# One of the last stores of a rotary-score kernel moved to a GpSimd transfer on fifteen DMA engines

## The chip, the cores and the metric

The kernel runs on one core of a Trainium2 chip. The metric is the device time of one execution in microseconds, as the median of several runs. A profile's span is about 2 us shorter than the time of the same run (797.1 against 798.9 for the kernel before).

## The reference

```python
# q, k: [16, 512, 16, 64] float32; cos, sin: [512, 32] float32
q_rot = concat([q1*cos - q2*sin, q1*sin + q2*cos])      # k_rot likewise
scores = np.einsum('bshd,bthd->bsht', q_rot, k_rot)     # [16, 512, 16, 512] float32
```

The output is 268 MB, the inputs 67 MB. The kernel has 64 steps, and each step makes 4 MB of the output: 128 rows of 32 KB from step 4 on, and the first four steps in quarters.

## The kernel before

The kernel plans all its instructions itself, with the waits worked out from keys that each instruction reads and writes. Three stage tiles of 4 MB take the scores. They lie in SBUF, on the chip, each over 128 partitions. ScalarE copies eight pieces per step into one, then SyncE stores it in one DMA transfer of 128 partitions (the code here and below is cut, with # ... where lines are left out):

```python
    NST_BUFS = 3
    stage = [pool.tile([P, H, S], fp32, name=f"st{n}") for n in range(NST_BUFS)]
    o_v = out.rearrange("b (p c) h t -> b c p h t", c=C)
    # ... in scores(i, p):
        plan.add(ACT, one(lambda: nc.scalar.copy(out=so, in_=si)), [("ps", y)], [("st", s, p)])
        # ...
        elif b > 0 and p == HP - 1:
            dma(SP, nc.sync, o_v[b, i % C], st, f"out{s}", reads=[("st", s, x) for x in range(HP)])
```

Four of the loads of q are already "relieved": 120 of their rows go through GpSimd on the fifteen DMA engines other than number 4, which is slower than the rest (1,246 ns for a row of 32 KB against 1,213 while compute runs; the prediction shows how it was found). A tiny transfer of five rows goes ahead of them, meant to move GpSimd's cursor past engine 4. In the trace, from 480 to 504 us, fifteen chains of packets then carry the 8 KB pieces, sixteen each, and the slow engine's chain carries none. Each row is named as two halves in reversed order. The last eight rows go on other transfers.

```python
    RELIEVED = {("q", 5): 0, ("q", 8): 1, ("q", 11): 2, ("q", 14): 3}
    SLOW = 4
    # ... in load(which, b):
        def halves(lo, hi, keys, sem):
            src = bass.AP(d.tensor, d.offset + lo * E + F, [(E, hi - lo), (-F, 2), (1, F)])
            # ... dst in the same form
            dma(POOL, nc.gpsimd, dst, src, sem, writes=keys)

        plan.add(POOL, None, (), rows)           # waits, then resets GpSimd's cursor
        if x % 2:
            move_cursor(8)
            halves(n, P, rest, f"rest{x}")       # eight odd rows, meant for engines 8 to 15
        move_cursor(SLOW + 1)
        halves(0, n, rows, f"part{x}")           # 120 rows on the engines other than 4
        if not x % 2:
            dma(SP, nc.sync, t[n:]..., d[n:], sem, writes=rest)   # or by SyncE, meant for engines 0 to 7
```

The trace names no engine, so the numbers are my count: 4 is the slow one, 0 to 7 are the eight that an 8-row transfer of SyncE uses, 8 to 15 the other eight. What the trace shows is that the 8-row load issued at 482.17 ended in eight increments, from 504.22 to 508.93 us, the last of them 0.6 us after the slow engine's for the store ahead (508.33), so I take the slow engine to be one of the eight. Which the others are was not shown.

## Time and profile before

| what | value |
|---|---|
| time, median of 3 runs | 798.52 us (797.91 to 799.9) |
| span of the profile | 797.1 us |
| busy: PE, ScalarE, VectorE, GpSimd | 86%, 71%, 68%, 1% |
| DMA queues of SyncE and of GpSimd, share of 16 engines' span | 96.5% and 2.4% |
| last four stores issued at | 745.83, 754.27, 763.51, 773.23 us |
| last increment of the last store | 794.86 us |

The prediction below shows the lines. A "last increment" is the last of the increments that a transfer makes on its semaphore (the last store made sixteen, from 786.93 to 794.86 us; I take each to be one engine's). The trace keeps every one of them, and every DMA packet with its queue, size and duration. It does not keep the engine's number.

### The profile page before, as it was taken

The numbers are of one execution on the slowest core, as the hardware profiler recorded it, in microseconds if no ns is written. First come the engines' busy times: TensorE is split into PE (matmuls) and PEld (weight loads), VectorE is DVE, ScalarE is ACT, GpSimd is POOL, SyncE is SP. The second block draws the span as 40 slices with busy tenths as digits, with TensorE's granted clock in tenths as the row PEclk, the third lists the DMA queues.
The fourth block names the chain that finished last, engine by engine and source line by source line (L and its number), as shares of the span: only waits on it lengthen the run. The fifth ranks groups of instructions, "written<-read, shape, count | busy, mean of one in ns | idle before, by whom it ended". The sixth has DMA issues, their size and how long they took to land.

```text
span 797.1 us, 8197 instructions
## 1 busy us (share of the span) xinstructions
PE 684.3 (86%) x3072; PEld 295.4 (37%) x3072; DVE 545.2 (68%) x516; ACT 562.4 (71%) x647; POOL 8.4 (1%) x18
## 2 busy tenths in 40 slices
PE   3989999897989979799797988979989699789960
PEld 2444443343333434344342433334334244334420
DVE  6999988575775868568585767757758488575400
ACT  3978886785767858578585866768667677678860
POOL 0000000000000000100000000000000100000000
PEclk9999999898998989989898999989989899899995
DMA  8999999999999999999999999999999999999995
GB/s 346 420 424 433 429 418 434 426 434 423 430 413 427 435 434 428 439 421 414 426 427 437 432 435 426 419 428 432 428 431 433 432 429 411 428 432 437 430 433 238
DMA packets 18513, 335.87 MB, mean 421 GB/s; under 512 B 2128, under 2 KB 3408, under 8 KB 4432
## 3 DMA queue, kind: packets, MB, share of 16 engines
q1 hardware_dynamic: 16832, 327.42, 96.5%
q0 software_dynamic: 1376, 8.13, 2.4%
q10 hardware_dynamic: 288, 0.13, 0.1%
q8 instruction: 6, 0.10, 0.0%
q14 instruction: 11, 0.09, 0.0%
HBM read 67.24 MB, written 268.44 MB: 421 GB/s over the span
## 4 chain that ended last, share of the span: by engine, by line
DMA 47%; PE 35%; DVE 8%; ACT 6%; issue 1%; ACTq 0%; DVEq 0%; SPq 0%
DMA out_dram<-st 47%; PE ps L409 27%; PE bank L360 9%; ACT st L418 6%; DVE st L335 3%; DVE part L335 2%; DVE k_sb L335 2%; DVE q_sb L335 1%; DMA st<-in_k_dram 1%; DVE kT L378 0%; DVE qT L378 0%; ACTq L110 0%; DVEq L110 0%; SPq L542 0%; SPq L513 0%
## 5 line engine op out<-in xcount | busy, mean ns | idle before, releaser
L418 ACT COPY st<-ps 128x1024 f32<-128x1024 f32 x512 | 495.5, 1018 | 196.7 <-DMA out_dram<-st 103.3
L409 PE MATMUL ps<-kT,qT 64*128 64x512 f32 x2048 | 542.9, 646 | 71.6 <-ACT st L418 71.6
L409 PEld LDWEIGHTS ps<-kT,qT 64*128 64x128 f32 x2048 | 182.0, 195 | 261.0 <-issue 134.2
L378 DVE COPY qT<-bank 128x512 f32<-128x512 f32 x118 | 81.6, 691 | 197.3 <-PE bank L360 197.3
L360 PEld LDWEIGHTS bank<-ident,q_sb 128*128 128x128 f32 x480 | 54.7, 150 | 101.5 <-issue 99.5
L360 PE MATMUL bank<-ident,q_sb 128*128 128x128 f32 x480 | 85.5, 305 | 1.0 <-DVE q_sb L335 1.0
L360 PEld LDWEIGHTS bank<-ident,k_sb 128*128 128x128 f32 x480 | 50.4, 141 | 94.5 <-DVE k_sb L335 43.1
L360 PE MATMUL bank<-ident,k_sb 128*128 128x128 f32 x480 | 78.6, 287 | 1.6 <-DVE k_sb L335 0.8
L378 ACT COPY kT<-bank 128x512 f32<-128x512 f32 x122 | 72.5, 597 | 6.7 <-PE bank L360 6.7
L335 DVE TENSOR_TENSOR part<-q_sb,ss_t 128x1024 f32<-128x1024 f32 x60 | 73.5, 1225 | 3.2
L335 DVE TENSOR_TENSOR k_sb<-k_sb,part 128x1024 f32<-128x1024 f32 x60 | 73.5, 1225 | 2.1
L335 DVE TENSOR_TENSOR k_sb<-k_sb,cos_t 128x1024 f32<-128x1024 f32 x60 | 73.5, 1225 | 2.0
L335 DVE TENSOR_TENSOR q_sb<-q_sb,cos_t 128x1024 f32<-128x1024 f32 x60 | 73.5, 1225 | 2.1
L335 DVE TENSOR_TENSOR part<-k_sb,ss_t 128x1024 f32<-128x1024 f32 x60 | 73.0, 1216 | 0.3
L335 DVE TENSOR_TENSOR q_sb<-q_sb,part 128x1024 f32<-128x1024 f32 x60 | 72.9, 1216 | 0.0
L360 PE MATMUL bank<-ident,st 128*128 128x128 f32 x64 | 10.8, 319 | 13.2 <-DVE st L335 13.2
L360 PEld LDWEIGHTS bank<-ident,st 128*128 128x128 f32 x64 | 8.2, 161 | 18.5 <-DVE st L335 16.7
L335 DVE TENSOR_TENSOR part<-st,ss_t 128x1024 f32<-128x1024 f32 x8 | 9.8, 1222 | 6.4 <-DMA st<-in_k_dram 6.0
L335 DVE TENSOR_TENSOR st<-st,part 128x512 f32<-128x512 f32 x16 | 11.1, 691 | 0.5
L237 POOL DMA_DIRECT2D scratch<-in_q_dram x6 | 3.6, 600 | 615.4 <-PE bank L360 615.4
L335 DVE TENSOR_TENSOR st<-st,cos_t 128x1024 f32<-128x1024 f32 x8 | 9.8, 1225 | 0.3
L378 ACT COPY qT<-bank 128x512 f32<-128x512 f32 x10 | 5.7, 615 | 3.5 <-PE bank L360 3.5
(11 smaller groups left out, 11.0 us busy)
## 6 DMA issues: line engine op xcount, KB each, us to landing
out_dram<-st SPq DMA_DIRECT2D x60, 4096.0 KB, 25.5
k_sb<-in_k_dram SPq DMA_DIRECT2D x15, 2048.0 KB, 27.1
q_sb<-in_q_dram SPq DMA_DIRECT2D x11, 2048.0 KB, 29.2
out_dram<-st SPq DMA_DIRECT2D x16, 1024.0 KB, 13.3
q_sb<-in_q_dram POOLq DMA_DIRECT2D x4, 1920.0 KB, 32.6
st<-in_k_dram SPq DMA_DIRECT2D x1, 1536.0 KB, 9.0
st<-in_q_dram SPq DMA_DIRECT2D x1, 1536.0 KB, 12.2
st<-in_k_dram SPq DMA_DIRECT2D x1, 512.0 KB, 5.0
```

The source lines that it names most:

```text
L237: plan.add(engine, one(lambda: e.dma_start(dst, src)), reads, writes, sem=sem, also=also)
L335: plan.add(DVE, one(lambda: nc.vector.tensor_tensor(o, a, b, op=op)), reads, writes, also=more)
L360: done = [nc.tensor.transpose(bank[:, x, :], srcs[x], ident) for x in range(4)]
L378: plan.add(engine, one(lambda: copy(out=dst, in_=src)), [("bank", m)], keys)
L409: nc.tensor.matmul(out=ps[:, r, :], lhsT=lhs[lo:hi, :], rhs=rhs[lo:hi, :], start=True, stop=True)
L418: plan.add(ACT, one(lambda: nc.scalar.copy(out=so, in_=si)), [("ps", y)], [("st", s, p)])
```

## The change

The intent is to spare engine 4 its share of one late store, since one engine, taken to be number 4, finishes the last store 3.59 us after all the others (794.86 against 791.27). The store of step 62, the last but one, takes the form of the relieved loads.

```diff
+        elif p == HP - 1 and i == NST - 2:
+            n, F, o = 120, H * S // 2, o_v[b, i % C]
+            keys = [("st", s, x) for x in range(HP)]
+            plan.add(POOL, None, keys[:2], ())
+            move_cursor(SLOW + 1)
+            v = st[:n].rearrange("p h t -> p (h t)")
+            src = bass.AP(v.tensor, v.offset + F, [(v.ap[0][0], n), (-F, 2), (1, F)])
+            dst = bass.AP(o.tensor, o.offset + F, [(o.ap[0][0], n), (-F, 2), (1, F)])
+            dma(POOL, nc.gpsimd, dst, src, "out_part", reads=keys)
+            dma(SP, nc.sync, o[n:], st[n:], f"out{s}", reads=keys)
         elif b > 0 and p == HP - 1:
```

(`move_cursor` also moves out of `load`, unchanged.)

More of the change, by code (lines that the diff above doesn't have):

```diff
@@ L262, with move_cursor @@
     SLOW = 4
+    def move_cursor(k):
+        y = tiny[0]
+        tiny[0] += 1
+        src = bass.AP(q.tensor, 512 * y, [(512, k), (64, 2), (1, 2)])
+        dst = scratch[:k, 4 * y : 4 * y + 4].rearrange("p (a b) -> p a b", a=2)
+        dma(POOL, nc.gpsimd, dst, src, "cursor", writes=[("scratch", y)])
     def load(which, b):
@@ L280, in load @@
         d = dram[which][b]
-        def move_cursor(k):
-            y = tiny[0]
-            tiny[0] += 1
-            src = bass.AP(q.tensor, 512 * y, [(512, k), (64, 2), (1, 2)])
-            dst = scratch[:k, 4 * y : 4 * y + 4].rearrange("p (a b) -> p a b", a=2)
-            dma(POOL, nc.gpsimd, dst, src, "cursor", writes=[("scratch", y)])
         def halves(lo, hi, keys, sem):
```

## The prediction

> **What bounds the kernel now.** I read the page first (parts 1, 2, 3 and 6), then the waits of SyncE, then the busy time of the last 40 us stretch by stretch, and last the trace's two raw records below the views: every DMA packet (queue, start, duration, bytes) and every semaphore increment that a DMA made.
>
> The page says that the DMA engines, not a compute engine, are full:
>
> ```profile
> PE 684.3 (86%) x3072; PEld 295.4 (37%) x3072; DVE 545.2 (68%) x516; ACT 562.4 (71%) x647; POOL 8.4 (1%) x18
> ...
> DMA  8999999999999999999999999999999999999995
> ...
> q1 hardware_dynamic: 16832, 327.42, 96.5%
> q0 software_dynamic: 1376, 8.13, 2.4%
> ...
> out_dram<-st SPq DMA_DIRECT2D x60, 4096.0 KB, 25.5
> ...
> q_sb<-in_q_dram POOLq DMA_DIRECT2D x4, 1920.0 KB, 32.6
> ```
>
> The reader should see a DMA row of nines with one exception that matters here: the last slice is a 5. The q0 row is GpSimd's own queue, already used by four loads of q in the form that the change now gives one store. The 60 big stores take 4 MB each.
>
> So what is the 5 at the end? The waits of SyncE from 745 us on, and the stretches of the end (columns: stretch, its length, busy time of PE, weight load, VectorE, ScalarE and GpSimd with instruction counts, clock, DMA share, GB/s):
>
> ```profile
> SPq L123 <- DMA out_dram<-st: 21.3, 1, 21.3
> ...
> 777.00:787.00 10.00, 0.00 (x0) 0.00 (x0) 0.00 (x0) 0.00 (x0) 0.00 (x0) 0.50 1.00 433
> 787.00:789.00 2.00, 0.00 (x0) 0.00 (x0) 0.00 (x0) 0.00 (x0) 0.00 (x0) 0.50 0.42 180
> 789.00:791.30 2.30, 0.00 (x0) 0.00 (x0) 0.00 (x0) 0.00 (x0) 0.00 (x0) 0.50 0.17 71
> 791.30:794.40 3.10, 0.00 (x0) 0.00 (x0) 0.00 (x0) 0.00 (x0) 0.00 (x0) 0.50 0.05 21
> ```
>
> After 773 us nothing computes. SyncE waits 21.3 us for the last store. Up to 787 all sixteen engines work (share 1.00), then they run dry one after another, and between 791.3 and 794.4 the share is 0.05, about one engine in sixteen. One engine alone sets the end.
>
> The semaphore increments give its size. The store of step 63 is issued at 773.23 and its sixteen increments land at 786.93, nine of them by 788.47, six more from 789.54 to 791.27, and the last at 794.86. The gap between the last two is **3.59 us**. The span ends at 797.11, so 2.25 us of closing work follow the landing.
>
> The packets tell why. From 705 us on they string into sixteen gapless chains. A 32 KB row of a store takes 1,213 ns on nearly all of them (about 1,209 from start to start), but on one it takes about 1,246 while compute runs, and 1,213 again once compute is over. That laggard loses 0.2 to 0.3 us per store: its increments for steps 57 to 61 are 9.8 to 10.0 us apart, those of the others 9.7. In the stretch from 480 to 504 us, where a relieved q load runs, fifteen chains carry 8 KB packets of q0 and the laggard carries none. So it is the engine that the code calls SLOW = 4.
>
> [...]
> - [...] fifteen chains with sixteen half-row packets each. [...] the 8-row load issued at 482.17 ended in eight increments from 504.22 to 508.93, most of them 0.6 us after an increment of the store ahead of it, and the last 0.6 us after the laggard's.
> - [...] one chain runs 8 KB of q0 and 32 KB of q1 in turn, a new q0 packet every 1.52 us (0.309 + 1.213), with no gap. Two queues on one engine only share its time.
> [...]
>
> **The change, part by part.**
> *Removed:* one store of 128 rows by SyncE at 763.51, which gives each engine 8 rows, 9.67 us.
> *Engine 4:* it loses 8 rows and keeps one of SyncE's eight. Seven rows of 1.21 us are 8.5 us. Before, it ended at 794.86; now 794.86 - 8.5 = 786.4 if nothing slows it. I add a malus: in the four relieved loads its 32 KB packets took up to about 1,500 ns while q0 ran, with a 4-byte q0 packet of its own between them. Its lag fell there only from 2.2 us (485.62 against 483.40) to 1.1 (534.35 against 533.25), much less than the share it was spared. Sixteen rounds of about 0.29 us are 4.6 us at the worst: 791.0.
> *Engines 0 to 3 and 5 to 7:* they keep their 8 rows, now as 16 packets of 16 KB, and gain one row of SyncE's. A 16 KB packet takes 611 ns (607.5 from start to start), so 16 x 607.5 - 8 x 1,209.5 = 44 ns more for the halves, and 1.21 us for the extra row: **+1.25 us**.
> *Engines 8 to 15:* +0.04 us.
>
> Which group holds the second-slowest engine? The 8-row load of 482 us shows that the slowest besides 4 was then in the group 0 to 7 (its store increment at 507.41 was followed by a row's at 508.00). The one behind it was in the other group, since the later relieved load, whose eight odd rows go to engines 8 to 15, moved the pair from 0.82 us apart (615.59, 614.77) to 0.06 (679.93, 679.87). At the end they are 791.27 and 791.22. So one of 0 to 7 ends at 791.25 + 1.25 = **792.5**, and that sets the end: later than 8 to 15 (791.3) and than engine 4 (786.4 to 791.0).
>
> *Added on GpSimd:* one cursor reset, one 5-row transfer of 80 bytes and the 120-row transfer, 0.6 + 0.75 us on an engine that is otherwise idle. The reset waits for two of the eight copies only, so it and the cursor transfer finish before the last copy. In the relieved load of 476.27 the first 8 KB packet started at 481.37, 5.1 us after the issue. Here that makes 763.5 + 5.1 = 768.6. The early engines run out of step 61 at about 767.1, so some of 8 to 15 may idle 1.5 us, but the ones that matter are busy with step 61 until about 771.4. The start is hidden there, with nearly 3 us to spare.
> *Not moved:* the copies of step 63 wait for the store of step 60, which lands at 765.70 before the new transfer starts. Step 63's store is still issued at 773.2.
>
> Sum: 794.86 - 792.5 = 2.35 us off the end. I give back 0.15 us for one more wait at the end and for the single stretched packets (0.3 to 0.6 us) that showed on some engines near the GpSimd loads. Net 2.2 us: 798.52 - 2.2 = **796.3 us**.
>
> **Rivals.**
> 1. *The eight odd rows were the wrong place.* This is inside my sum: without that row on 0 to 7 the end would be 791.3 and the gain 3.6 us. If the second-slowest engines are all in 8 to 15, the time is about 795.1. For it: the pair is only 0.06 us apart. Against: the increments of the odd row.
> 2. *GpSimd's start becomes the new wait.* If descriptors of a store came 8 us or more after the issue, instead of 5.1, late engines would idle too. Each microsecond beyond would come back, about 797 to 798.5. Against: the same number of descriptors (240) in the relieved loads, at 5.1 us.
> 3. *The laggard stays the bound,* because the q0 traffic slows it more than 0.3 us a packet: 797 to 798.5. For it: the 1,500 ns packets, up to 1,828 once. Against: with no loss it ends at 786.4, 6.1 us ahead of the 792.5 that sets the end, and sixteen packets would each have to lose 0.38 us.
> 4. *A shared limit* (the memory, not the engine) means that fifteen engines do sixteen engines' work no faster: 798.5. Against: a row takes 1,213 ns with sixteen engines active and the same when the laggard runs alone at 793 us.
>
> **Range and chances.** The runs of before spread by 2.0 us (797.91 to 799.9), as much as the effect, and the median of a few runs may be off by some 0.5. Rival 1 pulls to 795.1, rivals 2 and 3 to 797.5 or more. Eight times in ten I expect 795.2 to 797.6. A change of 2% is 16 us, while the only stretch touched has 3.6 us to give, and all that could be lost is a few microseconds of late start. So within 2% is nearly sure.
>
> **What would show it right or wrong.** In the changed profile the software queue should grow from 1,376 packets by about 290 and from 8.13 to 12.06 MB. The last increments should be one cluster ending near 792.5, with the slow engine's no longer last. The stretch from 791.3 to 794.4 should lose its lone engine. The first 16 KB packet of q0 should start near 768.6, SyncE's final wait should fall to about 19 us, and ScalarE's last copies should keep their times. I am wrong if the last increment still stands alone (rival 3), if the late chains show gaps between 768 and 773 (rival 2), or if rows take longer than 1,213 ns (rival 4).

## The result, and the profile after

The changed kernel takes **808.08 us** (median of 5 runs, 806.73 to 809.01) against 798.58 us before (5 runs). The ratio is 1.0114, 95% interval 1.0097 to 1.0131. It is the mean time of one kernel's runs over that of the other's of the same rounds, so not quite the ratio of the medians. Executions over 1.5% slower than the fastest of the same kernel are left out of the means. That is 9 us slower where 2 us faster was forecast.

The page of the changed kernel, with the lines that answer to those in the prediction:

```profile
PE 684.1 (85%) x3072; PEld 295.6 (37%) x3072; DVE 545.3 (68%) x516; ACT 562.7 (70%) x647; POOL 9.8 (1%) x20
...
DMA  8999999999999999999999999999999999999995
...
q1 hardware_dynamic: 16704, 323.49, 94.7%
q0 software_dynamic: 1680, 12.06, 4.1%
...
out_dram<-st POOLq DMA_DIRECT2D x1, 3840.0 KB, 37.6
```

The profiled run took 806.73 us, the shortest of the five, and the profiled run of before 798.9, so the traces differ by 7.8 us and the medians by 9.5.

Nothing looks amiss in the busy shares, and the queue of GpSimd carries what it should. The last line does: the 120 rows took 37.6 us from issue to landing, where a whole store of SyncE took 25.5 (median). SyncE's final wait grew from 21.3 to 28.1 us:

```profile
SPq L123 <- DMA out_dram<-st: 28.1, 1, 28.1
```

The same stretches of the end show where the time went, first before, then after (columns as in the prediction; the last two are the DMA share and GB/s):

```profile
767.00:777.00 10.00, 4.63 (x20) 1.41 (x20) 0.00 (x0) 6.20 (x7) 0.00 (x0) 0.93 0.99 429
777.00:787.00 10.00, 0.00 (x0) 0.00 (x0) 0.00 (x0) 0.00 (x0) 0.00 (x0) 0.50 1.00 433
787.00:797.00 10.00, 0.00 (x0) 0.00 (x0) 0.00 (x0) 0.00 (x0) 0.00 (x0) 0.50 0.14 59
```

```profile
767.00:777.00 10.00, 5.96 (x20) 2.19 (x20) 0.00 (x0) 6.27 (x7) 0.00 (x0) 0.84 0.98 287
777.00:787.00 10.00, 0.00 (x0) 0.00 (x0) 0.00 (x0) 0.00 (x0) 0.00 (x0) 0.50 1.00 305
787.00:797.00 10.00, 0.00 (x0) 0.00 (x0) 0.00 (x0) 0.00 (x0) 0.00 (x0) 0.50 0.74 280
```

This is the pair to learn from. (The view counts a packet, with its whole duration and size, in the stretch where it starts, so a share can pass 1.00.) From 767 to 787 us the share stays at 0.98 to 1.00, so the DMA engines count as busy, yet they move 287 and 305 GB/s instead of 429 and 433. They are occupied and slow. The packets say the same. After 764 us the 240 pieces of 16 KB took 914 ns each on average, against the 611 ns that I had reckoned with; half of them took 625 or less, 31 took 1,190 to 1,300, twice the time, and the longest took 2,524. The 199 rows of 32 KB in SyncE's queue went from 1,213 to 1,416 ns on average, the longest to 4,840. The extra, spread evenly, is 240 x 303 ns / 15 = 4.85 us on each of fifteen engines and 199 x 203 ns / 16 = 2.52 us on each of sixteen: 7.4 us together. The last increment moved by 7.8 us, from 794.86 to 802.62.

### The profile page after: what moved, and what is told of

It is laid out like the page before. It is cut to its first block, busy times and chain, and to the rows that moved or that the text cites. A ratio compares the mean times of both kernels' runs of the same rounds, so it can differ in the third digit from the quotient of the medians.

```text
span 804.9 us, 8200 instructions
## 1 busy us (share of the span) xinstructions
PE 684.1 (85%) x3072; PEld 295.6 (37%) x3072; DVE 545.3 (68%) x516; ACT 562.7 (70%) x647; POOL 9.8 (1%) x20
## 3 DMA queue, kind: packets, MB, share of 16 engines
q0 software_dynamic: 1680, 12.06, 4.1%
## 4 chain that ended last, share of the span: by engine, by line
DMA 48%; PE 35%; DVE 8%; ACT 5%; issue 1%; ACTq 0%; DVEq 0%; SPq 0%
DMA out_dram<-st 47%; PE ps L409 26%; PE bank L360 8%; ACT st L418 5%; DVE st L335 3%; DVE part L335 2%; DVE k_sb L335 2%; DVE q_sb L335 1%; DMA st<-in_k_dram 1%; DVE kT L378 0%; DVE qT L378 0%; ACTq L110 0%; DVEq L110 0%; SPq L553 0%; SPq L524 0%
## 6 DMA issues: line engine op xcount, KB each, us to landing
out_dram<-st POOLq DMA_DIRECT2D x1, 3840.0 KB, 37.6
```

## The experiments

Four theories stood at the start. *A:* a transfer of 120 rows gives each engine eight neighbouring rows instead of those it has in a transfer of 128, so that engines meet at one side of SBUF or of memory. *B:* GpSimd's queue is slow for stores. *C:* halves in reversed order are slow. *D:* two queues that store at the same time disturb each other.

Theory A rests on two assumptions of mine: that 120 rows are dealt out to the engines eight neighbours at a time, and that engines which are at neighbouring partitions at the same time hinder each other. *Port* below is a name for what such partitions share; which partitions share one is for m3 to show. The trace names neither engine nor partition of a packet, so the runs below test both assumptions by their effect.

### Who issues, how many rows, which pieces: e1_sync120, e2_gp128, e3_sync128h

e1 gives the 120 rows to SyncE, e2 gives 128 rows to GpSimd, e3 gives 128 rows in halves to SyncE:

```diff
-            dma(POOL, nc.gpsimd, dst, src, "out_part", reads=keys)      # e1; no cursor transfer
+            dma(SP, nc.sync, dst, src, "out_part", reads=keys)
-            n, F, o = 120, H * S // 2, o_v[b, i % C]                    # e2; no eight rows by SyncE
+            n, F, o = 128, H * S // 2, o_v[b, i % C]
                                                                         # e3: both
```

> The 120 rows of step 62 go by SyncE in the same two pieces a row, the last eight rows by SyncE as in the changed kernel; GpSimd does nothing at the end. Theory A (rows against engines: a transfer of 120 rows gives each engine eight neighbouring partitions instead of the partitions it has in a transfer of 128 rows, and engines then meet at one side of SBUF or of memory): as slow as the changed kernel, last increment at 802 us or later, pieces of 16 KB at 1,000 to 2,500 ns. Theory B (GpSimd's queue is slow for stores[...]): last increment near 795 to 797, pieces at 611 ns. Theory C (pieces of 16 KB in reversed order are slow): 802 or later. Theory D (two queues that both store get in each other's way): near 795 to 797.

> All 128 rows of step 62 go by one GpSimd transfer on all sixteen engines, in the same two pieces a row; no row by SyncE. Theory A (rows against engines): near the time of before, last increment at 795 to 797, pieces at 611 ns. Theories B (GpSimd's queue), C (pieces) and D (two queues): as slow as the changed kernel, last increment at 800 us or later with stretched pieces.

> All 128 rows of step 62 by SyncE, only cut in two pieces a row in reversed order. Theory C (pieces): slow, last increment at 800 us or later. Theories A, B and D: the time of before, last increment at 795, pieces at 611 ns.

| run | time, us (before) | ratio, 95% interval | last increment | 16 KB pieces, mean |
|---|---|---|---|---|
| e1: 120 rows, SyncE | 816.42 (798.91) | 1.022 (1.0203 to 1.0237) | 811.10 | 1,008 ns |
| e2: 128 rows, GpSimd | 798.44 (798.91) | 0.9988 (0.9972 to 1.0005) | 794.84 | 621 ns |
| e3: 128 rows, SyncE, halves | 799.36 (798.91) | 1.0001 (0.9981 to 1.002) | 796.05 | 611 ns |

The stretch from 777 to 787 us in e1, then in e2:

```profile
777.00:787.00 10.00, 0.00 (x0) 0.00 (x0) 0.00 (x0) 0.00 (x0) 0.00 (x0) 0.50 1.05 283
```

```profile
777.00:787.00 10.00, 0.00 (x0) 0.00 (x0) 0.00 (x0) 0.00 (x0) 0.00 (x0) 0.50 0.93 401
```

GpSimd is cleared by both: its queue with 128 rows is as fast as before, and SyncE with 120 rows is even slower than the changed kernel. Why one engine ends alone in e1, 9.5 us after the next (811.10 against 801.65), no run shows. The halves are cleared by e3, two storing queues by e2. What is left is the number of rows. In e2 the share is 0.93, but not from stretched packets: every piece that starts in that stretch takes 611 ns and every row 1,213. I take it that some engines had run out of rows by then. Only GpSimd's first three pieces, at 765.6 to 765.9, were much stretched (1,081 to 1,741 ns). The last increments come from one profile each; endings without a collision (before, e2, e3 and the three kernels with phases behind them) gave 794.2 to 796.1, so differences below 2 us are not read from them.

### Which side, SBUF or memory: m1_sync_stores

After the end of the kernel before, eight phases of further stores of the last stage run with nothing else beside them, each phase waiting for the one ahead. A phase is one store of 128 or 120 rows or sixteen stores of 8 rows, issued without a wait between them. The main lines of the edit, without the helpers and the whole stores before and after:

```diff
+    spread = [32 * g + r for g in range(4) for r in range(4)]   # 8 rows from here in steps of 4
+    packed = [8 * j for j in range(16)]                         # 8 neighbouring rows
+    run_phase(SP, nc.sync, [store(0, 128, 1, True)])            # True: in halves
+    run_phase(SP, nc.sync, [store(0, 120, 1, True)])
+    run_phase(SP, nc.sync, [store(x, 8, 4) for x in spread])
+    run_phase(SP, nc.sync, [store(x, 8, 1) for x in packed])
+    run_phase(SP, nc.sync, [store(y, 8, 1, to=(x, 4)) for x, y in zip(spread, packed)])
+    run_phase(SP, nc.sync, [store(x, 8, 4, to=(y, 1)) for x, y in zip(spread, packed)])
```

> The kernel before, and after its end eight more stores of the last stage, one after another, all by SyncE, nothing else running: 128 rows whole, 128 rows in two pieces, 120 rows in two pieces, sixteen transfers of 8 rows with partitions 4 apart, sixteen of 8 neighbouring partitions, then the two mixed forms (neighbouring partitions to rows 4 apart, and the other way round; they write wrong rows, which the last store of 128 rows puts right). Eight engines moving 16 rows each take at least 16 x 1.21 = 19.4 us. Theory A on the SBUF side: 12 us, 12 us, about 20 us, about 21 us, far more for neighbouring partitions (two sides for eight engines: up to 80 us), the same for neighbouring partitions to spread rows, and 21 us for spread partitions to neighbouring rows. Theory A on the memory side: the two mixed forms change places. Theories B and D: 120 rows take 12 us and all four 8-row forms 21 us. Theory C: both forms in two pieces about 20 us.

The stretches of the first seven phases, in the order of the text above, from the issue to the last increment (their second number is the length; the eighth, 128 rows again, took 11.11 us):

```profile
794.81:805.90 11.09, 0.00 (x0) 0.00 (x0) 0.00 (x0) 0.00 (x0) 0.00 (x0) 0.50 0.88 378
805.92:817.58 11.66, 0.00 (x0) 0.00 (x0) 0.00 (x0) 0.00 (x0) 0.00 (x0) 0.50 0.85 360
817.60:839.57 21.97, 0.00 (x0) 0.00 (x0) 0.00 (x0) 0.00 (x0) 0.00 (x0) 0.50 0.80 179
839.58:861.50 21.92, 0.00 (x0) 0.00 (x0) 0.00 (x0) 0.00 (x0) 0.00 (x0) 0.50 0.46 191
861.52:902.80 41.28, 0.00 (x0) 0.00 (x0) 0.00 (x0) 0.00 (x0) 0.00 (x0) 0.50 0.46 102
902.82:943.38 40.56, 0.00 (x0) 0.00 (x0) 0.00 (x0) 0.00 (x0) 0.00 (x0) 0.50 0.46 103
943.40:965.21 21.81, 0.00 (x0) 0.00 (x0) 0.00 (x0) 0.00 (x0) 0.00 (x0) 0.50 0.46 192
```

120 rows alone take 21.97 us where 128 rows in the same halves take 11.66: nearly twice the time for fewer bytes. In the 8-row forms the time goes with the SBUF partitions. Neighbouring partitions take 41.28 us, whether their rows of the output are neighbours or spread (40.56), and spread partitions take 21.92 or 21.81. So the collision is on the SBUF side, not in memory. The "up to 80 us" for neighbouring partitions was too much; why, no run shows. A row in the neighbouring form took 2,363 ns on average, in the spread form 1,242.

### Which partitions meet: m3_pairs

The same method with two rows at a time, on two engines, at a chosen distance. (The DMA share is 0.09 to 0.11 of sixteen engines for two rows, where two busy all the time would give 0.125, and 0.15 to 0.22 for four.) It is a direct test of which partitions meet. The main lines of the edit:

```diff
+    run_phase(SP, nc.sync, [store(x, 2, 1) for x in (0, 2, 32, 34)])
+    run_phase(SP, nc.sync, [store(x, 2, 4) for x in (0, 1, 2, 3)])      # and steps 8, 16, 32, 64
+    run_phase(SP, nc.sync, [store(x, 4, 1) for x in (0, 32)])           # and step 4
+    # then pairs and fours, 1 and 4 apart, as loads
```

> The kernel before, and after its end, one after another with nothing else running: four stores of two rows each on engines 0 and 1, the two rows always 1, 4, 8, 16, 32 or 64 partitions apart (for 1: 0 and 1, 2 and 3, 32 and 33, 34 and 35), then two stores of four rows 1 apart, two of four rows 4 apart, and the same as loads (pairs 1 and 4 apart, fours 1 and 4 apart). Theory A[...]: pairs 1 and 32 apart share a port, so 4 rows an engine take 8 x 1.21 = 9.7 us and about 12 with the start, the others 4.85 us and about 7; the fours 1 apart about 12, 4 apart about 5. For loads the same if writes collide, else the shorter times in all. If ports are no matter: all pairs about 7 us and all fours about 5.

The stretches of the pairs 1, 4, 8, 16, 32 and 64 apart, then the fours 1 and 4 apart:

```profile
805.33:816.66 11.33, 0.00 (x0) 0.00 (x0) 0.00 (x0) 0.00 (x0) 0.00 (x0) 0.50 0.11 23
816.68:823.36 6.68, 0.00 (x0) 0.00 (x0) 0.00 (x0) 0.00 (x0) 0.00 (x0) 0.50 0.09 39
823.37:829.81 6.44, 0.00 (x0) 0.00 (x0) 0.00 (x0) 0.00 (x0) 0.00 (x0) 0.50 0.10 41
829.83:836.35 6.52, 0.00 (x0) 0.00 (x0) 0.00 (x0) 0.00 (x0) 0.00 (x0) 0.50 0.09 40
836.37:848.08 11.71, 0.00 (x0) 0.00 (x0) 0.00 (x0) 0.00 (x0) 0.00 (x0) 0.50 0.11 22
848.10:854.45 6.35, 0.00 (x0) 0.00 (x0) 0.00 (x0) 0.00 (x0) 0.00 (x0) 0.50 0.10 41
854.47:865.78 11.31, 0.00 (x0) 0.00 (x0) 0.00 (x0) 0.00 (x0) 0.00 (x0) 0.50 0.22 23
865.80:869.93 4.13, 0.00 (x0) 0.00 (x0) 0.00 (x0) 0.00 (x0) 0.00 (x0) 0.50 0.15 63
```

Pairs 1 and 32 apart take 11.3 and 11.7 us, the others 6.4 to 6.7: of the distances tested, partitions 1 and 32 apart share a port, and those 4, 8, 16 and 64 apart do not. Fours 1 apart take 11.3 us, fours 4 apart 4.1. In all three forms on one port the same eight rows take about 11 us, with two engines at a time or with four. The rows themselves stretch: one takes 2,552 ns on average where two engines are at the port (pairs 1 apart), 4,960 where four are, and 1,221 to 1,226 where each is at its own. Divided by the engines at the port, that is one row in 1,276, 1,240 and 1,221 to 1,226 ns, so a port hands out about as much as one engine takes alone. As loads, pairs 1 and 4 apart took 11.52 and 7.49 us and fours 11.50 and 5.12, so writes into SBUF collide as well at distance 1, if the loads' rows in memory, which change with the partitions, do not matter there either; the mixed forms were run for stores only.

### GpSimd alone, and why the relieved loads looked clean: m2_gp_and_loads

The main lines of the edit (a whole store before, and the 120-row load by SyncE at the end, are left out):

```diff
+    move_cursor(SLOW + 1)
+    run_phase(POOL, nc.gpsimd, [store(0, 120, 1, True)])
+    run_phase(POOL, nc.gpsimd, [store(0, 128, 1, True)])
+    run_phase(SP, nc.sync, [fetch(0, 128, 1)])                   # loads of 16 KB rows
+    run_phase(SP, nc.sync, [fetch(x, 8, 4) for x in spread])
+    run_phase(SP, nc.sync, [fetch(x, 8, 1) for x in packed])
+    run_phase(POOL, nc.gpsimd, [fetch(0, 120, 1, True)])         # after a cursor transfer
```

> The kernel before, and after its end, one after another with nothing else running: a store of 128 rows by SyncE; 120 rows in two pieces by GpSimd on fifteen engines; 128 rows in two pieces by GpSimd; then loads of 16 KB rows: 128 rows by SyncE, sixteen of 8 rows with partitions 4 apart, sixteen of 8 neighbouring partitions, 120 rows by GpSimd (the form of the relieved loads), 120 rows by SyncE. Theory A: GpSimd's 120 rows about 22 us and its 128 rows about 12 to 13 us, as by SyncE. For the loads, if writes into SBUF collide like reads: 7, 12, 20 or more, 12, 11 us; if only reads collide: 7, 12, 12, 7, 7 us. Theory B (GpSimd's queue): both its stores about 20 us.

GpSimd's stores of 120 and 128 rows, then the load of 128 rows by SyncE and of 120 rows by GpSimd:

```profile
807.60:829.22 21.62, 0.00 (x0) 0.00 (x0) 0.00 (x0) 0.00 (x0) 0.75 (x2) 0.50 0.81 182
829.80:841.45 11.65, 0.00 (x0) 0.00 (x0) 0.00 (x0) 0.00 (x0) 0.75 (x1) 0.50 0.85 360
841.47:849.05 7.58, 0.00 (x0) 0.00 (x0) 0.00 (x0) 0.00 (x0) 0.00 (x0) 0.50 0.76 277
...
899.50:911.95 12.45, 0.00 (x0) 0.00 (x0) 0.00 (x0) 0.00 (x0) 0.76 (x2) 0.50 0.74 158
```

GpSimd's two stores take the times of SyncE's, 21.62 and 11.65 us. The loads of 8 rows took 14.13 us spread and 35.04 packed. And the relieved form of a load is slow by itself: 12.45 us against 7.58, with 8 KB pieces of 609 ns on average; by SyncE the same 120 rows took 12.80 us. Inside the kernel before, the same pieces took 310 ns on average, nearly all of them 309. What differs there is the company: each piece takes turns with a 32 KB row of a store, which reads SBUF, so an engine writes into SBUF for only 0.309 of every 1.52 us. Two engines at one port then want only two fifths of it by this estimate. This account of why the collision does not show there is argued from these durations; no run isolates it.

### Taking the collision away in place: e4b_apart, e6_own_ports, e7_own_ports_all

These three keep the changed kernel's engines, queue and output rows but read step 62 from other partitions, so their outputs are wrong on purpose. A first form of e4b, e4_apart, did not build: its transfer had more than three dimensions. e4b moves the halves in two GpSimd transfers; e6 and e7 move whole rows of 32 KB in three, so there the size of the pieces changes too (halves alone cost nothing in e3: ratio 1.0001). In e4b each engine is meant to read its eight rows from one partition, nine apart from the next engine's; I assumed that no two of these share a port, and m3 did not test those distances. In e6 the partitions are chosen so that, by my reckoning, each engine reads at the port where it also reads for SyncE's stores. In e7 the eight odd rows of SyncE are also read that way. The traces do not show who reads where, so these choices stand or fall with their effect.

```diff
 # shortened: p0 is the step from one partition to the next
 # e4b, for each half of the row (0 steps: the same partition eight times)
+  src = bass.AP(v.tensor, v.offset + half * F, [(9 * p0, 15), (0, 8), (1, F)])
 # e6 and e7, with the cursor reset and moved to 5 before the second
+  for first, engines in ((0, 4), (20, 3), (64, 8)):
+      src = bass.AP(v.tensor, v.offset + first * p0, [(4 * p0, engines), (0, 8), (1, 2 * F)])
 # e7
-  dma(SP, nc.sync, o[n:], st[n:], f"out{s}", reads=keys)
+  src = bass.AP(v.tensor, v.offset, [(4 * p0, 8), (1, 2 * F)])
```

> The changed kernel with one thing taken away: each of the fifteen engines reads its eight rows of step 62 from one partition of its own (0, 9, 18 and so on to 126[...]) instead of from eight neighbouring ones. The 120 rows written, the pieces of 16 KB, GpSimd's queue and SyncE's eight rows stay; it takes two GpSimd transfers of 15 x 8 pieces with a second cursor reset between, since one transfer cannot name it. The output of 120 rows of this step is wrong on purpose. Ports as the cause: the loss goes for the most part; last increment at 792.5 to 797 instead of 802.6, most pieces at 611 ns; some stretched ones stay[...]. If the number of rows, GpSimd or memory were to blame: 802 or later, as in the changed kernel.

> The changed kernel, but GpSimd's fifteen engines read for step 62[...] one partition each,[...] in three GpSimd transfers with whole rows of 32 KB. Rows written, engines and queue as in the changed kernel; the eight odd rows by SyncE still come from partitions 120 to 127[...]. The output is wrong on purpose. Ports as the cause: what was left of the loss[...] (798.5) goes too, except for the odd rows: last increment at 792.5 to 796, nearly all of GpSimd's rows at 1,213 ns. If something else of GpSimd's transfer costs the rest: about 798 as before.

> The same, and the eight odd rows of SyncE are read[...] (partitions 0, 4 to 28).[...] Wrong output on purpose. This is the situation that the prediction assumed: last increment near 792.5 (791.3 + 1.25), time about 2 us below the kernel before, engine 4 not the last. If ports are not all of it, it stays above 794.9.

| run | time, us (before) | ratio, 95% interval | last increment | GpSimd's pieces, mean | SyncE's 32 KB rows, mean |
|---|---|---|---|---|---|
| changed kernel | 808.08 (798.58) | 1.0114 (1.0097 to 1.0131) | 802.62 | 914 ns (611) | 1,416 ns |
| e4b | 802.38 (798.38) | 1.0046 (1.0031 to 1.0062) | 798.52 | 748 ns (611) | 1,370 ns |
| e6 | 799.96 (798.63) | 1.0027 (1.0002 to 1.0051) | 794.46 | 1,258 ns (1,213) | 1,269 ns |
| e7 | 796.79 (798.63) | 0.999 (0.9969 to 1.0012) | 792.12 | 1,236 ns (1,213) | 1,215 ns |

In brackets behind the means stands the undisturbed duration of that size. The stretch from 777 to 787 us in e4b, e6 and e7, one fence each:

```profile
777.00:787.00 10.00, 0.00 (x0) 0.00 (x0) 0.00 (x0) 0.00 (x0) 0.00 (x0) 0.52 1.01 374
```

```profile
777.00:787.00 10.00, 0.00 (x0) 0.00 (x0) 0.00 (x0) 0.00 (x0) 0.00 (x0) 0.50 0.97 413
```

```profile
777.00:787.00 10.00, 0.00 (x0) 0.00 (x0) 0.00 (x0) 0.00 (x0) 0.00 (x0) 0.50 1.00 429
```

From 305 GB/s in the changed kernel the rate climbs to 374, 413 and 429. By the reckoning behind the three forms, the meetings are taken away one kind at a time: fifteen engines with each other, GpSimd's reads with SyncE's stores, and the eight odd rows with both. e4b fell short of its expectation (798.52, outside 792.5 to 797). Its SyncE rows still took 1,370 ns on average, against 1,269 in e6. That fits meetings of GpSimd's reads with SyncE's stores that stretch the rows of both; no run shows more of it. e6's runs fall into two groups, 798.4 and 801.5 us, which I cannot explain; its median is therefore worth little, and its trace is of a run of the faster group (798.47). In e7 the last increment is at 792.12, where the prediction had reckoned 792.5 without collisions; endings repeat less well than that, so 0.4 us of agreement is in part luck. By its times e7 is not clearly faster (one of its four runs took 799.12, the others 796.14 to 797.18), so the agreement rests on the trace and on the medians.

### Relief where it costs nothing: v1_fifth_load, v2_gp_rest

Engine 4 can be spared by one more relieved load instead.

```diff
-    RELIEVED = {("q", 5): 0, ("q", 8): 1, ("q", 11): 2, ("q", 14): 3}
+    RELIEVED = {("q", 5): 0, ("q", 8): 1, ("q", 11): 2, ("q", 14): 3, ("q", 15): 4}   # v1; v2: 5
```

> The kernel before with a fifth relieved load (q of batch 15), the form that kept engine 4 off 120 rows without hurting: a candidate for a faster kernel. A relieved load cut engine 4's lag by about 1.1 us net before, and made the other engines 0.6 to 1 us later. So the last increment at 793.5 to 795 instead of 794.9, a gain of 0 to 1.4 us; a loss of 1 us or more would say that loads in this form also cost something.

> The fifth relieved load with its eight odd rows by GpSimd on engines 8 to 15 instead of by SyncE on 0 to 7. In the version with SyncE's odd rows engine 4 landed at 792.67 and the slowest of the others at 792.63. Engine 4 no longer takes a row of 0.61 us, so it should land near 792.1, and the slowest of 8 to 15, at 791.2 before, near 791.8: a gain of 0.5 us on that version, 2.5 to 3 us on the kernel before. If the second pair of GpSimd transfers costs as much as it saves: the same as that version.

v1 takes **796.81 us** (796.5 to 797.52, 6 runs; before 799.24 us, 11 runs), ratio 0.9971 (0.9954 to 0.9987). It is correct and 0.3% faster than the kernel before. Its last increment is at 792.67, better than expected, and the one before it at 792.63: no engine ends alone any more. In the stretch that held one lone engine before, no row starts any more; the last two start just ahead of it and end at 792.2 and 792.3:

```profile
789.00:791.30 2.30, 0.00 (x0) 0.00 (x0) 0.00 (x0) 0.00 (x0) 0.00 (x0) 0.50 0.17 71
791.30:794.40 3.10, 0.00 (x0) 0.00 (x0) 0.00 (x0) 0.00 (x0) 0.00 (x0) 0.50 0.00 0
```

v2, in which GpSimd moves the odd rows, meant for engines 8 to 15, takes 796.64 us (before 798.38), ratio 0.9976 (0.9963 to 0.999), last increment 792.53. The further 0.5 us that I expected does not show.

## Why the prediction was wrong

**The step that failed** is the cost of the moved rows: "16 x 607.5 - 8 x 1,209.5 = 44 ns more for the halves", and with it "+0.04 us" for engines 8 to 15. A duration was carried over from rows that did not hinder each other (1,213 ns in stores of 128 rows) to rows read at partitions that do (in m3 a row took 1,221 to 1,226 ns alone at a port and 2,552 where two engines met). The pieces took 914 ns on average instead of 611, and SyncE's rows beside them 1,416 instead of 1,213. That is 7.4 us an engine where 0.04 stood. m1 and m3 show the meeting by itself (41.28 against 21.92 us, 11.3 against 6.7), and e7, meant to remove it, gets the forecast end (792.12).

**Rival 4 named a shared limit and was put aside for a reason that did not bear on it.** A row does take 1,213 ns both with sixteen engines active and alone, but all those rows came from one assignment of rows to engines, that of 128 rows. The evidence was silent on a different one. The limit is also not "the memory" but the SBUF side (m1: 41.28 and 40.56 us for neighbouring partitions, wherever their rows go in the output, 21.92 and 21.81 for spread ones).

**The relieved loads, from which the prediction took the form, gave no warning.** Their 309 ns in the trace were right, but they held for a writing stream that fills a fifth of the time. Alone, the same form takes 609 ns a piece (m2). That the share of the time makes the difference is argued above and not shown.

**The odd rows.** Besides the 1.21 us that was counted, they collide: from e6 to e7, where only the partitions change that they are read from, the last increment drops from 794.46 to 792.12 and SyncE's rows from 1,269 to 1,215 ns on average.

**What held.** GpSimd's start is hidden: the first 16 KB piece started at 767.08, earlier than the 768.6 reckoned. The queue of GpSimd grew by 304 packets (about 290 expected) to 12.06 MB. The end is worth 2.2 to 2.7 us if engine 4's lag goes: v1 and e7 landed at 792.67 and 792.12, against 794.86. Rivals 2 and 3 played no part that the runs show; rival 1, other engines for the odd rows of the store, was not run. The time did stay within 2%, but that was luck: the reason given was that only a few microseconds could be lost, and nine were. Each failed marker was listed in advance: the last increment moved later, the final wait became 28.1 us instead of 19, and rows took longer than 1,213 ns.

**What held only in part.** The last copies did not quite keep their times: step 63's store was issued at 774.22, against 773.23, because two of its copies waited 0.35 and 0.58 us for matmuls. The engines had rows to move meanwhile (DMA share 0.98), so this does not explain the loss.

**Open.** Why one engine, taken to be number 4, needs 1,246 ns for a row while compute runs was not looked into. Nor was how the 7.4 us split between reads that meet inside GpSimd's transfer and reads that meet SyncE's, other than by the steps from e4b to e7. Some 16 KB packets of loads took up to 1,708 ns in the kernel before, many of them after a relieved load but some, at 112 us, before any; no run explains them.

## What to carry to other kernels

When a transfer changes its number of rows, a duration per packet from the old form need not hold: 120 rows instead of 128 took 21.97 us against 11.66, in the same halves. Work out which partitions are read at the same time; in m3 those 1 and 32 apart got in each other's way, those 4, 8, 16 and 64 apart did not. A DMA share of 1.00 with fewer GB/s than before (305 against 433 here) says that packets take longer, and such a meeting is one thing to look for. A form that is harmless in one direction and at a fifth of the traffic (309 ns a piece) may cost nearly twice its time when it fills the engines (609 ns alone; 21.97 us against 11.66 as a store), so measure it alone before moving it.
